# A gated retention and sparse-attention block on one core: another order for the first stage

## The chip, the cores and the metric

The kernel runs on one core of a Trainium2 chip. The metric is the device time of one execution in microseconds (us); lower is better. The kernel before took 1618.48 us, the median of three runs (1618.11 to 1619.36).

## The reference

One decoder layer on x, 512 tokens of 2048 channels, in fp32. What the change touches is the beginning and the last step:

```python
mod = silu(c) @ w_ada + b_ada                 # one row of 6144 from w_ada, 2048 x 6144
shift, scl, gate = split(mod, 3)
h = rmsnorm(x, g_norm) * (1 + scl) + shift
(..., n_kc, ..., n_ks, ..., n_kw, ...) = split(h @ w_in, ...)
y_ret = retention(rope(r_q), rope(r_k), r_v) * silu(r_g)
y_nsa = nsa_attention(rope(n_q), n_kc, n_vc, rope(n_ks), n_vs, rope(n_kw), n_vw, ...) * silu(n_g)
merged = sigmoid(m_a) * (y_ret @ w_up_ret) + sigmoid(m_b) * (y_nsa @ w_up_nsa)
out = rmsnorm(x + gate * (merged @ w_out), g_final)
```

So nothing can be multiplied by w_in before shift and scl of at least the first channels are known, and these need the whole contraction over c with w_ada.

## The kernel before

The 2048 channels stand on 16 tiles of 128 partitions (kk = 0 to 15), the 512 tokens beside each other. Each factor of a product is split into a high and a low part in fp32r (whi and wlo of the weights, hhi and hlo of h), so that one tile pair takes three matmuls of 128 x 512: hi by hi, hi by lo, lo by hi. Below, such a matmul is called a product.

**Weights.** All weights come over SyncE's queue (SP) in slices of half a megabyte, 128 x 1024, in the order of a list, `plan`; `load` issues what lies up to 12 places ahead (L236), as soon as one of its buffers is free: five `raw` tiles, and two pairs in a pool that is used later for something else. `split` (L251) copies a slice to whi on ScalarE (ACT, L261) and subtracts it to wlo on VectorE (DVE, L262), three of each at a time. Small constants come over GpSimd's queue (POOL) at the start.

**The first stage.** Sixteen squares (DVE, L271) are summed by 16 matmuls against ones (`ssq`, L272); from that comes 1/rms of each token (`rstd_of`, L274, and `rstd_rows`, L289). Beside this, w_ada runs through TensorE (PE) in eight chunks j, each of 512 columns: shift and scl of the two tiles kk = 2j and 2j + 1. A chunk has eight half-megabyte items, two to a batch: `ada_batch` (L316) makes four matmuls of 128 x 512 in fp32 into `pa` (L324). At a chunk's end `xn` (L856) multiplies two tiles of x by 1/rms, `ada_rows` copies `pa` out (ACT), `ada_cols` (L331) turns the row into columns by four matmuls (`misc`, L311; "the column sums" below), adds the constants (`sh`, L337 to L339), makes h (L344), casts it to hhi (ACT, L345) and subtracts to hlo (DVE, L346).

**What fills the gaps.** Two groups of w_in are multiplied meanwhile: group 0 (the keys and values to be compressed) in four PSUM banks, by `Group.steps` (L394, products at L414), 24 products to an item; and group 1 (four key columns of 128, "keys"), item by item into a free bank and added to an fp32 tile `kacc` (`k_step`, L870: products L879, add L885; at the last item the add is L889 and the rope of the column follows it, L486 to L494). The keys come in half-width items of their own array (`w_half`): an item serves two columns over four kk, 12 products to a step. `queue_item` puts steps into a queue `todo` with the batch from which they may run (4j + 2 for chunk j), and `pop` takes steps worth 12 products after each batch: one chunk's products run during the next chunk's sums. `early_splits` splits the next items, up to three ahead, when they are loaded; after the last chunk it runs before every step and takes the first item of the next group (group 2, the values, "v"; its products stand at L414 too, with the weights as the moving side named first, g<-whi,hhi). After the fourth step of that rest `make_gates` (L352) follows: 16 matmuls (`pbg`, L357), and after the eighth 4 more (`pgt`, L364) and the step `gate` on DVE (L368).

**The end.** `out_evac` (L1050) takes the last product's blocks from PSUM, adds the residual, sums the squares (ACT, L1056), and after the fourth block of a row makes its 1/rms by a chain of small steps and writes the row.

Of the kernel before, what the change touches and what calls it, by code (L numbers as in the profile page):

```python
# [85 lines left out]
def block_kernel(ctx: ExitStack, tc: tile.TileContext, t_in, out):  # L86
# [34 lines left out]

    def load_const(name, shape, dt=F32, q=None):
        t = cst.tile(shape, dt, name=f"c_{name}")
        (q or nc.gpsimd).dma_start(t, t_in[name])
        return t
# [6 lines left out]
    gn = load_const("gn", [P, NK])  # L132
    bsh = load_const("bsh", [P, NK])
    bsc = load_const("bsc", [P, NK])
    rtmp = bigt("rtmp")
    bgw = rtmp[:, 7, :].rearrange("p (k c) -> p k c", k=NK)
    nc.gpsimd.dma_start(bgw, t_in["bgw"])
    invc = load_const("invc", [P, 2])
    posb = wk.tile([P, S], I32, tag="pT", bufs=3, name="posb")
    nc.gpsimd.dma_start(posb, bcast(t_in["pos"], S))  # L140
# [29 lines left out]
    def startup_items(j):  # L170

        its = [("w", "in", 0, j)]
        if j % 2:
            its += [("h", 0, j // 2), ("h", 1, j // 2)]
        return its
# [22 lines left out]
    SRC = {"a": "w_ada", "h": "w_half", "in": "w_in", "c": "w_c1", "g": "w_gate", "up_r": "w_ur", "up_n": "w_un", "out": "w_o"}  # L198
    raws, splits = {}, {}
    loaded = [0]  # L200
    w_idx = [i for i, it in enumerate(plan) if it[0] in "wh"]
# [13 lines left out]
    free = {"raw": RAWB, "kv": 2}  # L215
    pair_left = {}

    def load(idx):

        while loaded[0] < min(idx + 12, len(plan)):  # L220
            i = loaded[0]
            it = plan[i]
            if it[0] == "a" and it[2] % 4 >= 2:
                if it[2] % 2 == 0:
                    if not free["kv"]:
                        break
                    free["kv"] -= 1
                    t = kvp.tile([P, 2, 1024], F32, tag="kv", name=f"raw{i}")
                    nc.sync.dma_start(t, t_in["w_ada"][it[1], it[2]:it[2] + 2].rearrange("s p f -> p s f"))
                    raws[i], raws[i + 1] = t[:, 0, :], t[:, 1, :]  # L230
            else:
                if not free["raw"]:
                    break
                free["raw"] -= 1
                r = wp.tile([P, 1024], F32, tag="raw", bufs=RAWB, name=f"raw{i}")
                nc.sync.dma_start(r, raw_src(it))  # L236
                raws[i] = r
            loaded[0] += 1

    def take(i):  # L240

        if i not in raws:
            load(i)
        it = plan[i]
        if it[0] == "a" and it[2] % 4 >= 2:
            free["kv"] += it[2] % 2
        else:
            free["raw"] += 1
        return raws.pop(i)

    def split(upto):  # L251

        while split_ptr[0] < min(upto + 1, len(w_idx)):
# [8 lines left out]
            nc.vector.tensor_tensor(lo, r, hi.bitcast(F32), op=OP.subtract)  # L262
# [5 lines left out]
    for kk in range(NK):  # L268
        sq = wk.tile([P, 512], F32, tag="ev", bufs=4, name=f"sq{kk}")
        xk = xT[kk // 8][:, kk % 8, :]  # L270
        nc.vector.tensor_tensor(sq, xk, xk, op=OP.mult)  # L271
        nc.tensor.matmul(ssq, ones, sq, start=kk == 0, stop=kk == NK - 1)  # L272
# [15 lines left out]

    def rstd_rows():  # L289

        for t in range(NT):
            nc.vector.scalar_tensor_tensor(rtmp[:, 1, :P], ssq[:, t * P:(t + 1) * P], 1.0, ident, op0=OP.mult,
                                           op1=OP.mult, accum_out=st4[:, t:t + 1])
        rstd_of(st4, st4, 1.0 / D, "rr", [P, NT])
        prs = sbank("prs")
        for t in range(NT):
            c = slice(t * P, (t + 1) * P)
            nc.vector.tensor_scalar(rtmp[:, 2, c], ident, st4[:, t:t + 1], None, op0=OP.mult)
# [4 lines left out]
    h_hi = [bigt(f"hhi{a}", F32R) for a in range(2)]  # L303
    h_lo = [bigt(f"hlo{a}", F32R) for a in range(2)]
# [11 lines left out]
    def ada_batch(idx, j, b):  # L316


        load(idx + 1)
        rs = [take(idx + n).rearrange("p (a b) -> p a b", a=2) for n in range(2)]  # L320
        if b == 0:
            pa[j] = tbank(f"pa{j}")
        for u in range(4):
            nc.tensor.matmul(pa[j][32 * u:32 * u + 32, :], sc32[:, 4 * b + u, :], rs[u // 2][:, u % 2, :],  # L324
                             start=b == 0, stop=b == 3)

    def ada_rows(j):
        rows = wk.tile([P, 512], F32, tag="p", bufs=3, name=f"rows{j}")
        nc.scalar.copy(rows, pa.pop(j))
        return rows  # L330

    def ada_cols(j, rows):

        for q in range(4):
            misc_mm(pcol[:, j, q:q + 1], rows[:, q * P:(q + 1) * P], ones[:, 0:1])
        sh = wk.tile([P, 4], F32, tag="sh", bufs=2, name=f"sh{j}")
        nc.vector.tensor_tensor(sh[:, 0:2], pcol[:, j, 0:2], bsh[:, 2 * j:2 * j + 2], op=OP.add)  # L337
        nc.vector.tensor_tensor(sh[:, 2:4], pcol[:, j, 2:4], bsc[:, 2 * j:2 * j + 2], op=OP.add)
        nc.vector.scalar_tensor_tensor(sh[:, 2:4], sh[:, 2:4], 1.0, gn[:, 2 * j:2 * j + 2], op0=OP.add, op1=OP.mult)  # L339
        for u in range(2):  # L340
            kk = 2 * j + u
            a, k8 = divmod(kk, 8)
            h = xT[a][:, k8, :]
# [43 lines left out]
    class Group:  # L387
# [6 lines left out]
        def steps(self, items):  # L394
# [4 lines left out]
            ks = [(self.kk + n * per + u, i, u) for n, i in enumerate(items) for u in range(per)]  # L399
            self.kk += per * len(items)  # L400
            last = self.kk == self.nk

            def step(t):
# [12 lines left out]
                if t == nt - 1:  # L416
# [14 lines left out]
    def run_group(grp, idx, n, between=None, tail=2):  # L431
# [3 lines left out]
        while done < n:  # L435
            if plan[idx][0] not in "wh":
# [9 lines left out]
        while idx < len(plan) and plan[idx][0] not in "wh":  # L446
# [409 lines left out]
    xn_next = [0]  # L856

    def xn(n):

        for _ in range(n):  # L860
            kk = xn_next[0]
            if kk < NK:
                h = xT[kk // 8][:, kk % 8, :]
                nc.vector.tensor_tensor(h, h, rstd, op=OP.mult)
                xn_next[0] += 1

# [4 lines left out]
    def k_step(i, n, t):  # L871
# [3 lines left out]
        for u in range(4):  # L875
            kk = 4 * n + u
            f = slice(u * 256 + (t % 2) * P, u * 256 + (t % 2) * P + P)
            for m, (l, r) in enumerate(((whi[:, f], hhi(kk)), (whi[:, f], hlo(kk)), (wlo[:, f], hhi(kk)))):
                nc.tensor.matmul(b, l, r, start=u == 0 and m == 0, stop=u == 3 and m == 2)  # L879
        if t % 2:  # L880
            splits.pop(i)
        if n == 0:
            nc.scalar.copy(kacc[t], b)
        elif n < 3:
# [11 lines left out]
    def early_splits(idx):  # L896
        while len(splits) < 3 and split_ptr[0] < len(w_idx) and w_idx[split_ptr[0]] <= idx and w_idx[split_ptr[0]] < loaded[0]:
            split(split_ptr[0])

    def queue_item(i, ready):  # L900

        it = plan[i]
        if it[0] == "w":
            todo.extend((ready, 6, f) for f in g0.steps([i]))
        else:
            todo.extend((ready, 12, lambda t=t: k_step(i, it[2], t)) for t in (2 * it[1], 2 * it[1] + 1))
# [263 lines left out]
```

## Time and profile before

| | |
|---|---|
| median of three runs | 1618.48 us |
| the profiled execution, its own time | 1619.62 us |
| its span in the profile | 1617.9 us |
| PE busy | 1588.0 us (98%) |
| DVE, ACT, POOL busy | 712.6 (44%), 489.2 (30%), 33.9 us |
| DMA | 252.54 MB, 156 GB/s over the span |
| granted clock, mean | 0.996 |

The profiled execution is 1.14 us above the median, and 1.72 us of its time lie outside the span. PE is busy nearly throughout; its idle time adds up to 30 us, and the slices of the page show it in the first slice (0 to 40 us) and the last.

### The profile page before, as it was taken

The numbers are of one execution on the slowest core, as the hardware profiler recorded it, in microseconds if no ns is written. First come the engines' busy times: TensorE is split into PE (matmuls) and PEld (weight loads), VectorE is DVE, ScalarE is ACT, GpSimd is POOL, SyncE is SP. The second block draws the span as 40 slices with busy tenths as digits, with TensorE's granted clock in tenths as the row PEclk, the third lists the DMA queues.
The fourth block names the chain that finished last, engine by engine and source line by source line (L and its number), as shares of the span: only waits on it lengthen the run. The fifth ranks groups of instructions, "written<-read, shape, count | busy, mean of one in ns | idle before, by whom it ended". The sixth has DMA issues, their size and how long they took to land.

```text
span 1617.9 us, 18828 instructions
## 1 busy us (share of the span) xinstructions
PE 1588.0 (98%) x7502; PEld 1266.3 (78%) x7502; DVE 712.6 (44%) x1238; ACT 489.2 (30%) x719; POOL 33.9 (2%) x68
## 2 busy tenths in 40 slices
PE   7999999999999999999999999999999999999997
PEld 2566777888888888778888888888888888778886
DVE  5454533345534344542245343332221566654444
ACT  1223313234433534432333333332222222222223
POOL 2000000000000000000001000000001000010000
PEclk9999999999999999999999999999999999999999
DMA  9886354323323313213544554333335777884322
GB/s 373 325 312 222 112 172 152 105 91 106 103 72 98 105 59 98 92 59 111 172 143 134 178 179 147 122 124 124 112 112 167 271 230 236 260 297 182 104 79 105
DMA packets 88217, 252.54 MB, mean 156 GB/s; under 512 B 9248, under 2 KB 18528, under 8 KB 86976
## 3 DMA queue, kind: packets, MB, share of 16 engines
q1 hardware_dynamic: 80048, 235.71, 42.5%
q0 software_dynamic: 7504, 13.53, 2.7%
q10 hardware_dynamic: 576, 2.10, 0.3%
q8 instruction: 59, 0.97, 0.2%
q14 instruction: 30, 0.25, 0.0%
HBM read 224.03 MB, written 27.26 MB: 155 GB/s over the span
## 4 chain that ended last, share of the span: by engine, by line
PE 90%; DVE 4%; DMA 3%; ACT 2%; issue 1%; SPq 0%; ACTq 0%; DVEq 0%
PE g L414 58%; PE o L414 11%; PE u L414 6%; PE g L879 2%; PE o L719 2%; PE sc L682 2%; PE pa L324 2%; PE tp L705 1%; PE ssq L272 1%; PE phid L603 1%; DMA raw<-in_w_ada 1%; DVE wlo L262 1%; DMA raw<-in_w_un 1%; DMA raw<-in_w_ur 1%; PE o L716 1%
## 5 line engine op out<-in xcount | busy, mean ns | idle before, releaser
L262 DVE TENSOR_TENSOR wlo<-raw,whi 128x1024 fp32r<-128x1024 f32 x246 | 297.9, 1223 | 487.0 <-ACT whi L261 486.9
L414 PE MATMUL g<-hhi,whi 128*128 128x512 f32 x1088 | 438.2, 403 | 0.0
L414 PE MATMUL g<-hhi,wlo 128*128 128x512 f32 x1088 | 424.8, 390 | 1.6 <-DVE wlo L262 1.6
L414 PE MATMUL g<-hlo,whi 128*128 128x512 f32 x1088 | 424.1, 390 | 0.0
L261 ACT CAST whi<-raw 128x1024 fp32r<-128x1024 f32 x246 | 255.0, 1048 | 499.8 <-PE g L414 229.0
L414 PEld LDWEIGHTS g<-hhi,whi 128*128 128x128 f32 x1088 | 204.7, 188 | 56.2 <-issue 11.6
L414 PEld LDWEIGHTS g<-hhi,wlo 128*128 128x128 f32 x1088 | 204.5, 188 | 46.4 <-DVE wlo L262 2.5
L414 PEld LDWEIGHTS g<-hlo,whi 128*128 128x128 f32 x1088 | 204.8, 188 | 42.9 <-issue 1.4
L414 PE MATMUL g<-whi,hhi 128*128 128x512 f32 x320 | 133.8, 418 | 0.0
L414 PE MATMUL g<-wlo,hhi 128*128 128x512 f32 x320 | 124.9, 390 | 1.2 <-DVE wlo L262 1.2
L414 PE MATMUL g<-whi,hlo 128*128 128x512 f32 x320 | 125.0, 391 | 0.0
L414 PE MATMUL o<-whi,mhi 128*128 128x512 f32 x240 | 95.0, 396 | 0.0
L414 PE MATMUL o<-wlo,mhi 128*128 128x512 f32 x240 | 93.5, 390 | 0.0
L414 PE MATMUL o<-whi,mlo 128*128 128x512 f32 x240 | 93.4, 389 | 0.0
L414 PEld LDWEIGHTS g<-wlo,hhi 128*128 128x128 f32 x320 | 60.2, 188 | 16.7 <-issue 2.4
L414 PEld LDWEIGHTS g<-whi,hhi 128*128 128x128 f32 x320 | 60.1, 188 | 15.8 <-issue 3.2
L414 PEld LDWEIGHTS g<-whi,hlo 128*128 128x128 f32 x320 | 60.0, 188 | 13.0
L685 DVE CUSTOM_DVE_ANT_0 p<-sc,c_mask 128x128 f32<-128x128 f32 (+3 forms) x64 | 31.2, 488 | 85.3 <-PE sc L682 85.2
L706 ACT COPY pT<-tp 128x128 f32<-128x128 f32 (+3 forms) x64 | 27.3, 426 | 114.6 <-PE tp L705 114.4
L687 ACT ACTIVATE p<-p,sm 128x128 f32<-128x128 f32 (+3 forms) x64 | 36.1, 563 | 75.6 <-DVE sm L685 75.5
L414 PEld LDWEIGHTS o<-wlo,mhi 128*128 128x128 f32 x240 | 45.0, 188 | 10.6 <-issue 1.0
L719 PEld LDWEIGHTS o<-pT,vt 128*128 128x128 f32 x320 | 44.8, 190 | 10.9 <-issue 5.3
(238 smaller groups left out, 1699.8 us busy)
## 6 DMA issues: line engine op xcount, KB each, us to landing
raw<-in_w_in SPq DMA_DIRECT2D x176, 512.0 KB, 3.7
raw<-in_w_ada SPq DMA_DIRECT2D x32, 512.0 KB, 7.7
raw<-in_w_ada SPq DMA_DIRECT2D x16, 1024.0 KB, 8.1
raw<-in_w_gate SPq DMA_DIRECT2D x32, 512.0 KB, 4.7
raw<-in_w_o SPq DMA_DIRECT2D x32, 512.0 KB, 4.4
raw<-in_w_c SPq DMA_DIRECT2D x16, 512.0 KB, 4.1
raw<-in_w_un SPq DMA_DIRECT2D x16, 512.0 KB, 5.1
sg<-ma_d SPq DMA_DIRECT2D x32, 256.0 KB, 3.5
```

What stands on the lines that cost most here:

```text
L261: nc.scalar.copy(hi, r)
L262: nc.vector.tensor_tensor(lo, r, hi.bitcast(F32), op=OP.subtract)
L272: nc.tensor.matmul(ssq, ones, sq, start=kk == 0, stop=kk == NK - 1)
L324: nc.tensor.matmul(pa[j][32 * u:32 * u + 32, :], sc32[:, 4 * b + u, :], rs[u // 2][:, u % 2, :], start=b == 0, stop=b == 3)
L414: nc.tensor.matmul(self.banks[t], l, r, start=kk == 0 and n == 0, stop=kk == self.nk - 1 and n == 2)
L603: nc.tensor.matmul(hid[64 * v:64 * v + 64, :], wins[v, s][:, i, :], craw[v][:, i, :], start=s == 0 and i == 0, stop=s == 7 and i == 3)
L682: nc.tensor.matmul(b[:, :n], qT[:, h, t], res["kT"][:, 2 * br + g, :n], start=True, stop=True)
L685: nc.vector.tensor_tensor_reduce(p[:, :n], b[:, :n], mask[:, 512 - n:], -SCALE, 3.0e38, OP.add, OP.min, sm[:, 0:1])
L687: nc.scalar.activation(p[:, :n], p[:, :n], AF.Exp, bias=sm[:, 0:1], scale=-1.0, accum_out=sm[:, 1:2])
L706: nc.scalar.copy(pT[:, :n], b[:, :n])
L719: nc.tensor.matmul(o[:, r * P:(r + 1) * P], res["v"][:, m, 256 * br + P * g:256 * br + P * g + P], pT[:, m * P:(m + 1) * P], start=k == fi ...
L879: nc.tensor.matmul(b, l, r, start=u == 0 and m == 0, stop=u == 3 and m == 2)
```

## The change

The first stage is written anew.

- **Buffers.** 17 slots of half a megabyte: the five `raw` tiles, four from the two pairs, and eight halves of two large tiles (`xw`) which later become the second half of h (hhi1, hlo1); these eight are given up from the first item of chunk 3 on. `load` runs up to 20 items ahead. The constants that are not needed at once come over SP's queue at the start of chunk 2.
- **First chunk.** Chunk 0 is summed in two halves, of one tile kk each, and the first half's h is made before the second half's sums are run. Its eight items come as 16 DMAs of 256 KB whose rows are 4 x 512 bytes.
- **1/rms.** Of four squares three are on ACT; they are added in pairs on DVE, so that 8 matmuls sum them. The chain to 1/rms stands right behind.
- **Batches.** Chunks 0 and 1 in four batches, the others in two of four items (eight matmuls each).
- **Keys.** Full-width items, two kk for four columns: four steps of 6 products to an item. `w_half` is gone; as many bytes come with `w_in`.
- **Order of the queue.** `pop` takes 24 products after the first batch of a chunk, 18 after the second, and 6 ahead of the column sums. `early_splits` splits up to the item `lim`, which after the last chunk is the last item of group 1.
- **The end.** In `out_evac` the sum of three blocks' squares is made at the third block, so that after the fourth two small DVE steps fewer follow.

The core of the diff:

```diff
+    BATCH = [[2, 2, 2, 2]] * 2 + [[4, 4]] * 6
     for j in range(8):
-        for b in range(4):
-            plan += [("a", j, 2 * b), ("a", j, 2 * b + 1)]
-            if j:
-                plan += startup_items(j - 1)[b:b + 1]
-    plan += startup_items(7)
+        for u in range(8):
+            plan.append(("a", j, u))
+            if (j, u) == (0, 3):
+                plan.append(("w", "in", 0, 0))
+        plan += [("w", "in", g, j) for g in range(2) if j or g]
...
-    free = {"raw": RAWB, "kv": 2}
+    xw = [kvp.tile([P, 2, 1024], F32, tag="kv", name=f"xkv{a}") for a in range(2)]
+    xw += [bigt(f"xw{a}").rearrange(...) for a in range(2)]
+    slots = deque([("raw", None)] * RAWB + [("kv", xw[a][:, u, :]) for a in range(2) for u in range(2)]
+                  + [("big", xw[2 + a][:, u, :]) for a in range(2) for u in range(4)])
...
+            if it[0] == "a" and it[1] == 0:
+                hb, n = divmod(it[2], 4)
+                for u in range(2):
+                    nc.sync.dma_start(r[:, 512 * u:512 * u + 512].rearrange("p (k c) -> p k c", k=4),
+                                      t_in["w_ada"][0, 2 * n + u].rearrange("p (k c) -> p k c", k=4)
+                                      [:, :, P * hb:P * hb + P])
...
-        nc.vector.tensor_tensor(sq, xk, xk, op=OP.mult)
-        nc.tensor.matmul(ssq, ones, sq, start=kk == 0, stop=kk == NK - 1)
+        for u in range(3):
+            nc.scalar.activation(sq[u], xk[u], AF.Square)
+        nc.vector.tensor_tensor(sq[3], xk[3], xk[3], op=OP.mult)
+        for u in (0, 2):
+            nc.vector.tensor_tensor(sq[u], sq[u], sq[u + 1], op=OP.add)
+            nc.tensor.matmul(ssq, ones, sq[u], start=a == 0 and u == 0, stop=a == 3 and u == 2)
...
+    def early_splits():
+        while len(splits) < 3 and w_idx[split_ptr[0]] < min(loaded[0], lim[0]):
+            split(split_ptr[0])
...
+            if b == nb - 1:
+                rows = ada_rows(j)
+                lim[0] = idx + 1
+            pop(24 // nb if j == 1 else 48 // nb if b < nb - 1 else 42 // nb - 6)
...
+        pop(6)
+        cols_mm(j, rows, (0, 1))
+        cols_h(j, (0, 1))
+        for i in (idx, idx + 1):
+            queue_item(i)
+        idx += 2
+        lim[0] = idx
     gates_finish = None
-    for i in range(idx, idx + 3):
-        queue_item(i, 0)
-    idx += 3
     i = 0
     while todo:
-        load(idx - 3)
-        early_splits(idx)
-        todo.popleft()[2]()
+        load(idx - 2)
+        early_splits()
+        todo.popleft()[1]()
...
-                sm = wk.tile([P, 1], F32, tag="fsm", bufs=2, name=f"fsm{t}")
-                nc.vector.tensor_reduce(sm, acc[:, t, :], axis=AX.X, op=OP.add)
-                rstd_of(rf[:, t:t + 1], sm, 1.0 / D, "fr", [P, 1])
+            if j == 2:
+                nc.vector.tensor_reduce(v, acc[:, t, 0:3], axis=AX.X, op=OP.add)
+                nc.vector.tensor_scalar(v, v, 1.0 / D, EPS, op0=OP.mult, op1=OP.add)
+            if j == 3:
+                nc.vector.scalar_tensor_tensor(v, acc[:, t, 3:4], 1.0 / D, v, op0=OP.mult, op1=OP.add)
```

`cols_mm` and `cols_h` do what `ada_cols` did, for one tile kk or for two; `cols_h` begins with the two multiplies of `xn`.

How the order moves is read from the programs' instructions, engine by engine. First, TensorE at a chunk's end in the kernel before: the column sums (misc) of a row, the next chunk's first sums (pa), and then a key step (g_0_2).

```order
L311 MATMUL misc<-ones,rows_892 128x1 x4
L324 MATMUL pa_910<-raw_818,rtmp 32x512 x2
L324 MATMUL pa_910<-raw_841,rtmp 32x512 x2
L879 MATMUL g_0_2_919<-hhi_180,whi_824 128x512
L879 MATMUL g_0_2_919<-hlo_182,whi_824 128x512
```

And the same place in the changed program, at the end of chunk 6; g_3_5 is the last step of chunk 5's keys, g_0_196 the first of chunk 6.

```order
L336 MATMUL misc<-ones,rows_950 128x1 x4
L353 MATMUL pa_0_1012<-raw_937,rtmp 32x512 x2
L353 MATMUL pa_0_1012<-raw_939,rtmp 32x512 x2
L353 MATMUL pa_0_1012<-xkv_118,rtmp 32x512 x2
L353 MATMUL pa_0_1012<-xkv_119,rtmp 32x512 x2
L907 MATMUL g_3_5_1025<-hhi_759,whi_902 128x512
...
L907 MATMUL g_3_5_1025<-hhi_759,wlo_903 128x512
L453 MATMUL g_0_196<-hhi_759,whi_952 128x512
```

Before, a whole chunk of older products stood behind the column sums; now eight sums and six products do, and then those products that need the tiles just made.

Second, VectorE where the first stage gives way to group v, in the kernel before; wlo_1112 and wlo_1204 are the low parts of v's first and second item, kacc_193 to kacc_196 the four key columns.

```order
L368 TENSOR_SCALAR gate_185<-gates,c_valid_101 128x8
L262 TENSOR_TENSOR wlo_1112<-raw_975,whi_1111 128x1024
L889 TENSOR_TENSOR kacc_193<-g_0_3_1115,kacc_193 128x512
L492 TENSOR_TENSOR kT<-kacc_193,cosT 128x512
...
L889 TENSOR_TENSOR kacc_196<-g_3_3_1178,kacc_196 128x512
L492 TENSOR_TENSOR kT<-kacc_196,cosT 128x512
L493 TENSOR_TENSOR rotk_1192<-rotk_1192,sinT 128x512
L494 TENSOR_TENSOR kT<-kT,rotk_1192 128x512
L262 TENSOR_TENSOR wlo_1204<-raw_1019,whi_1203 128x1024
```

The same place in the changed program; wlo_1257 is the low part of v's first item.

```order
L917 TENSOR_TENSOR kacc_203<-g_2_7_1216,kacc_203 128x512
L531 TENSOR_TENSOR kT<-kacc_203,cosT 128x512
L532 TENSOR_TENSOR rotk_1224<-rotk_1224,sinT 128x512
L533 TENSOR_TENSOR kT<-kT,rotk_1224 128x512
L405 TENSOR_SCALAR gate_193<-gates,c_valid_96 128x8
L917 TENSOR_TENSOR kacc_204<-g_3_7_1237,kacc_204 128x512
L531 TENSOR_TENSOR kT<-kacc_204,cosT 128x512
L532 TENSOR_TENSOR rotk_1245<-rotk_1245,sinT 128x512
L533 TENSOR_TENSOR kT<-kT,rotk_1245 128x512
L270 TENSOR_TENSOR wlo_1257<-raw_1118,whi_1256 128x1024
L270 TENSOR_TENSOR wlo_1261<-raw_1122,whi_1260 128x1024
```

The low part of v's first item stood ahead of the four ropes and now stands behind them, and so does the step `gate`.

Third, TensorE from the last sum of squares to the first product, in the changed program (pa_0_235 and pa_4_284 are the two halves of chunk 0).

```order
L288 MATMUL ssq<-sq_161,ones 128x512
L353 MATMUL pa_0_235<-raw_205,rtmp 32x256 x4
...
L336 MATMUL misc<-ones,rows_256 128x1 x2
L317 MATMUL prs<-rtmp,ones 128x128 x4
L353 MATMUL pa_4_284<-xkv_118,rtmp 32x256 x8
L453 MATMUL g_0_196<-hhi_189,whi_258 128x512
```

Before, the sums of two whole chunks but for one batch stood ahead of the first product; now there are those of chunk 0 less two of its items.

## Rows read from the trace of the kernel before

**Rows 1.** The page: busy us of the engines, share of the span, instructions.

```profile
PE 1588.0 (98%) x7502; PEld 1266.3 (78%) x7502; DVE 712.6 (44%) x1238; ACT 489.2 (30%) x719; POOL 33.9 (2%) x68
```

**Rows 2.** PE timeline, 20 to 64 us: start, length, line, operation, count.

```profile
22.81 1.92 PE L324 MATMUL pa<-raw,rtmp 128*32 128x512 f32 x16
39.15 0.80 PE L414 MATMUL g<-hhi,whi 128*128 128x512 f32 x1
61.85 1.06 PE L324 MATMUL pa<-raw,rtmp 128*32 128x512 f32 x8
```

**Rows 3.** Groups by line, PE, 7 to 61.85 us: count | busy us, mean ns.

```profile
L414 PE MATMUL g<-hhi,whi 128*128 128x512 f32 x16 | 7.2, 453 | 0.0
```

**Rows 4.** Windows: start:end, length, PE, PEld, DVE, ACT, POOL busy, granted clock, DMA share, GB/s.

```profile
32.00:34.00 2.00, 0.14 (x4) 0.14 (x8) 1.15 (x2) 0.78 (x2) 0.00 (x0) 1.00 1.04 422
36.00:38.00 2.00, 1.93 (x6) 0.38 (x8) 1.93 (x5) 0.00 (x0) 0.00 (x0) 0.50 1.02 420
40.00:42.00 2.00, 2.00 (x7) 1.54 (x7) 0.00 (x0) 0.00 (x0) 0.00 (x0) 0.64 1.03 420
871.00:872.00 1.00, 1.00 (x6) 0.83 (x5) 0.19 (x1) 0.98 (x2) 0.00 (x0) 1.00 1.01 353
872.00:873.00 1.00, 1.00 (x6) 0.84 (x5) 1.00 (x1) 1.00 (x1) 0.00 (x0) 1.00 0.84 242
```

**Rows 5.** Chain that ended last, 160 to 187 us: start, length, what.

```profile
164.74 0.70 DVE kacc L889
...
178.26 1.23 DVE wlo L262
...
179.53 5.51 PE g L414 x23
```

**Rows 6.** DVE timeline, 0 to 40 us; in brackets idle time before, and its releaser.

```profile
6.37 2.50 DVE L271 TENSOR_TENSOR sq<-xT 128x512 f32<-128x512 f32 x4 [3.54 <-DMA xT<-in_xT]
17.43 1.89 DVE L271 TENSOR_TENSOR sq<-xT 128x512 f32<-128x512 f32 x3 [0.69 <-DMA xT<-in_xT]
23.00 0.29 DVE L292 SCALAR_TENSOR_TENSOR rtmp<-ssq,ident 128x128 f32<-128x128 f32 x1 [2.82 <-PE ssq L272]
28.04 1.29 DVE L864 TENSOR_TENSOR xT<-xT,rtmp 128x512 f32<-128x512 f32 x2
```

**Rows 7.** PE timeline, 60 to 205 us.

```profile
78.86 1.05 PE L311 MATMUL misc<-ones,rows 128*128 128x1 f32 x8 [1.16 <-ACT rows L329]
112.11 0.95 PE L311 MATMUL misc<-ones,rows 128*128 128x1 f32 x8
151.73 3.64 PE L357 MATMUL pbg<-xT,rtmp 128*32 128x512 f32 x32
161.69 0.47 PE L879 MATMUL g<-hhi,whi 128*128 128x512 f32 x1
172.47 0.39 PE L879 MATMUL g<-hhi,wlo 128*128 128x512 f32 x1
```

**Rows 8.** DVE and ACT timeline, 110 to 120 us, around the column sums of 112.11.

```profile
113.52 1.28 DVE L864 TENSOR_TENSOR xT<-xT,rtmp 128x512 f32<-128x512 f32 x2
114.72 0.15 DVE L337 TENSOR_TENSOR sh<-misc,c_bsh 128x2 f32<-128x2 f32 x1
115.75 0.62 ACT L345 CAST hhi<-xT 128x512 fp32r<-128x512 f32 x1 [5.78 <-DVE xT L344]
118.24 0.69 DVE L346 TENSOR_TENSOR hlo<-xT,hhi 128x512 fp32r<-128x512 f32 x1 [0.68 <-ACT hhi L345]
```

**Rows 9.** DMA queues, 0 to 60 us: packets, MB, share of 16 engines.

```profile
q0 software_dynamic: 592, 0.94, 5.6%
```

**Rows 10.** ACT and DVE timeline, 1564 to 1618 us.

```profile
1567.77 2.36 DVE L262 TENSOR_TENSOR wlo<-raw,whi 128x1024 fp32r<-128x1024 f32 x2 [0.25 <-ACT whi L261]
1609.32 0.63 ACT L1056 ACTIVATE oe<-xr 128x512 f32<-128x512 f32 x1 [1.35 <-DVE xr L1055]
1611.49 0.16 DVE L281 TENSOR_TENSOR frv<-frv,fry 128x1 f32<-128x1 f32 x1
```

More of the change, by code (lines that the diff above doesn't have):

```diff
@@ L243, in take, with split @@
             load(i)
[L244 to L248, printed above, removed]
+        slots.append(held.pop(i))
         return raws.pop(i)
-    def split(upto):
+    def split(upto, part=None):
         while split_ptr[0] < min(upto + 1, len(w_idx)):
@@ L328, in ada_rows, with cols_mm @@
+    def ada_rows(j, w=512):
         rows = wk.tile([P, 512], F32, tag="p", bufs=3, name=f"rows{j}")
-        nc.scalar.copy(rows, pa.pop(j))
+        nc.scalar.copy(rows[:, :w], pa.pop(j)[:, :w])
         return rows
[L332 to L341, printed above, removed]
+    def cols_mm(j, rows, us):
+        for n, q in enumerate([u + 2 * v for v in range(2) for u in us]):
+            misc_mm(pcol[:, j, q:q + 1], rows[:, n * P:(n + 1) * P], ones[:, 0:1])
@@ new lines, in cols_h @@
+    def cols_h(j, us, between=None):
+        xn(j, us)
+        u0, n = us[0], len(us)
+        sh = wk.tile([P, 4], F32, tag="sh", bufs=2, name=f"sh{j}{u0}")
+        k0 = 2 * j + u0
+        nc.vector.tensor_tensor(sh[:, 0:n], pcol[:, j, u0:u0 + n], bsh[:, k0:k0 + n], op=OP.add)
+        nc.vector.tensor_tensor(sh[:, 2:2 + n], pcol[:, j, 2 + u0:2 + u0 + n], bsc[:, k0:k0 + n], op=OP.add)
+        nc.vector.scalar_tensor_tensor(sh[:, 2:2 + n], sh[:, 2:2 + n], 1.0, gn[:, k0:k0 + n], op0=OP.add, op1=OP.mult)
+        for u in range(n):
+            kk = k0 + u
@@ L392, in __init__, with steps @@
             self.kk, self.k0 = 0, k0
-        def steps(self, items):
+        def steps(self, items, us=None):
             nt = len(self.banks)
@@ L445, in run_group @@
                 items = []
-        while idx < len(plan) and plan[idx][0] not in "wh":
+        while idx < len(plan) and plan[idx][0] != "w":
             between(idx, plan[idx])
@@ L908, in pop @@
-    def pop(batch, room):
-        while todo and room > 0 and todo[0][0] <= batch:
-            _, n, f = todo.popleft()
+        if it[2] == 0:
+            todo.extend((6 if us is None else 3, f) for f in g0.steps([i], us))
+        else:
+            todo.extend((6, lambda t=t: k_step(i, it[3], t)) for t in range(4))
+    def pop(room):
+        while todo and room > 0:
+            early_splits()
+            n, f = todo.popleft()
             f()
             room -= n
-        return room
@@ L916, in block_kernel @@
[L916 to L934 removed]
+    i_w0 = plan.index(("w", "in", 0, 0))
@@ new lines, in block_kernel @@
+    load(0)
+    for b in range(2):
+        ada_batch(2 * b, 0, 2 * b, 2)
+    rows = ada_rows(0, 256)
+    part = []
+    split(0, part)
+    cols_mm(0, rows, (0,))
+    rstd_rows()
+    cols_h(0, (0,))
+    part[0]()
+    queue_item(i_w0, (0,))
+    ada_batch(5, 0, 4, 2)
+    pop(6)
+    ada_batch(7, 0, 6, 2)
+    rows = ada_rows(0, 256)
+    pop(6)
+    cols_mm(0, rows, (1,))
+    cols_h(0, (1,))
+    queue_item(i_w0, (1,))
+    queue_item(9)
+    idx = lim[0] = 10
+    for j in range(1, 8):
+        if j == 2:
+            for dst, src in late:
+                nc.sync.dma_start(dst, src)
+        s0 = 0
+        nb = len(BATCH[j])
+        for b, n in enumerate(BATCH[j]):
+            load(idx)
+            ada_batch(idx, j, s0, n)
+            idx += n
+            s0 += n
+            if b == nb - 1:
+                rows = ada_rows(j)
+                lim[0] = idx + 1
+            pop(24 // nb if j == 1 else 48 // nb if b < nb - 1 else 42 // nb - 6)
+            for _ in range(2):
+                if j > 2 and tables:
+                    tables.popleft()()
+        pop(6)
+        cols_mm(j, rows, (0, 1))
[4 more added lines that the diff above has]
+        lim[0] = idx
```

190 lines of the change are left out of this document (94 added, 96 removed).

## The prediction

> **What bounds the kernel now.** I read the page first: TensorE is busy 1588.0 of 1617.9 us [rows 1], so a change gains only where PE waits, some 30 us in all, or loses by making it wait anew. The PE timeline says where: the first product starts at 39.15, and at 61.85, when chunk 3's sums begin, 48 products are done (16 of each of three kinds) [rows 2, 3]. The windows tell why: between 32 and 34 us PE works 0.14 of 2 us while the DMA runs at its full 422 GB/s [rows 4]. From 61.85 on PE runs almost without a gap (the column sums at 78.86 wait 1.16 us [rows 7]) until the chain of waits shows the change of group: v's second product waits for the low part of its second item, behind four ropes on VectorE, until 179.53 [rows 5].
>
> The sum is made as a timetable of the changed stage, as far as the instant that answers to that 179.53, the second product of v's second item. Behind it both programs do the same until the end.
>
> **Start.** The first quarter of x is there at 6.37, the last at 17.43 [rows 6]. The 0.94 MB of constants [rows 9] no longer mix with it: three quarters, 3.15 MB, at 420 GB/s [rows 4] take 7.5 us, so 13.9. From there three squares on ACT, priced as the same operation at the end, 0.63 each [rows 10], a last square and add on DVE and two passes of PE give 17.4 for the end of ssq, 5.5 earlier than the 23.00 of before [rows 6]. The chain to 1/rms takes 28.04 - 23.00 = 5.0 us as now [rows 6]: 22.5. Then one tile's multiply (half of 1.29, 0.65), the three steps at sh (0.45 from start to start) and the scaling (0.55), and the cast, 0.62 [rows 6, 8]: first product at 24.8, 14.3 earlier.
>
> **To chunk 3's sums, by PE.** From the order, 90 products are done by then instead of 48. A product costs 0.228 us: from 161.69 to 172.47 lie 47 [rows 7], 10.78 / 47 = 0.229, pauses included. 90 make 20.5. A batch of four matmuls into pa takes 1.06 [rows 2] and 0.14 of changing over; what is left of chunk 0 and the 32 of chunks 1 and 2 make 10.4. Three lots of column sums at 0.5, 0.95 and 0.95 [rows 7]: 2.3. That is 24.8 + 33.2 = 58.0. To it come waits, 1.05 at each of three boundaries (below), 3.15, and the clock. PE will have idled for most of the time from 17.4 to 24.8. Before, after the idle stretch at 32 to 36 us, the granted clock was 0.50 from 36 to 38 and 0.64 on the mean from 40 to 42, so half (1.2 GHz) up to about 41.4 [rows 4]: 5.4 busy us at half rate, a loss of 2.7. The price here lies between 0 and 2.7; PE has somewhat more to do in its idle stretch than it had then, so I take 2.3. Chunk 3's sums begin at 63.4.
>
> **The same, by DMA.** x (4.2 MB), the constants and 34 half-megabyte items make 22.95 MB. Of these 4.2 MB come in rows of 512 bytes; the nearest rows, loads of such rows late in the kernel, moved 353 GB/s in a full window [rows 4]: 11.9 us. The other 18.75 MB at 420: 44.7. Started at about 3.9 (6.37 less one quarter's 2.5) they are in at 60.5. PE is the later of the two. So the change stands 42 products ahead and 1.5 us behind: 8.0 us ahead at this point. `w_half` becoming `w_in` moves no byte and costs nothing.
>
> **Chunks 3 to 7.** Each has 48 products (10.94), two batches of eight sums (2 x 2.07) and column sums (0.88, the row's 0.95 less what overlaps): 15.96. Now the boundary. Counted from the start of the column sums at 112.11, sh starts 2.6 us later (114.72), for an add and the multiplies of xn (1.28) stand ahead of it on DVE; the first hhi is cast at 115.75 (done at +4.3), the second hlo is done at +6.8 [rows 7, 8]. Before, a chunk of older products hid all that. In the new order only eight sums (2.07) and six products (1.37) follow the 0.88 of the column sums, so the first product that needs the new tiles comes at +4.3, that which needs the second tile's at +5.0. With the steps closed up, as no other work is mixed in, I put the second hhi at +5.45 and the second hlo at +6.2: two waits of about 0.5, 1.05 us a boundary. By the row as it stands it is 1.7, and 0 if sh starts a microsecond earlier. 5 x 17.01 = 85.05: the last column sums are through at 148.45.
>
> **The rest of the queue.** 54 products: 6; then a wait without the sums as cover, 1.05 + 2.07 = 3.1; 24 of group 0; `pbg`, 3.64 [rows 7]; and 6 of the first key column. 148.45 + 1.37 + 3.1 + 5.47 + 3.64 + 1.37 + 0.2 until DVE has the bank = 163.6. Before, the first rope's add started at 164.74 [rows 5]. Of the 8.0 us 6.9 are given back by here.
>
> **Into group v.** Before, v's first item was split ahead of the ropes, and its 24 products covered the last of them. Now its low part stands behind the fourth rope. From the first add to the product behind such a subtraction it took 179.53 - 164.74 = 14.79 [rows 5]; `gate`, a small step like the 0.16 of [rows 10], adds 0.25 with its gaps. So v's **first** item gets its second product at 163.6 + 15.05 = 178.6, and the second item's follows 24 products (5.47) later, at 184.1: 4.6 behind the 179.53 of before. PE has 18 key products, `pgt` and one of v in these 15 us, some 5.3, and idles the other 9.7. What is late next is nothing: DVE subtracts v's second and third item while PE multiplies the first.
>
> **Clock.** Such idling brought half rate once [rows 4]; its price is again 0 to 2.7, and I take 2.0. The Trainium skill, "TensorE: Matmul & The Clock Gate", section "HAM oscillation — how this bites in real kernels", says that waits between bursts of matmuls put TensorE back to half rate; the one stretch in these rows agrees, and by it the price would be the whole 2.7, the sum 1625.7.
>
> **End.** Two DVE steps of 0.16 (0.2 with their gaps) go from the last chain [rows 10]: -0.4. Two such steps are put ahead of the low parts at 1567.77 for each of four rows of blocks, 1.5 us on DVE; whether PE then waits no row shows: 0 to +1.5, nearer 0, for those parts are made several items ahead. I take +0.3, together -0.1.
>
> **Sum.** +4.6 + 2.0 - 0.1 = +6.5, against the profiled execution's 1619.62, which is 1.14 above the median of 1618.48: **1625.0**. What a measurement of this kernel can tell from no change is about 0.2%, 3.2 us; so 1615.2 to 1621.7 is the same.
>
> **Rivals.**
> - *h is ready in time* (faster, or the same). If sh starts within 1.6 us of the column sums, the waits at the boundaries vanish: 2.9 up to chunk 3, where the DMA's 60.5 then bounds, 5.25 in chunks 3 to 7, 1.05 behind them, together 9.2. That gives 1615.8, and 1613.8 if the clock keeps its full rate in the tail. For it: in the row the add and xn stand ahead of sh, and a scheduler's order could let them run before the sums end. Against it: the keys' adds double in number (each item now has four columns for every chunk), and the row shows sh 1.7 us behind the end of the column sums. Faster decides from a gain of 9.8: 0.18, and 0.12 for the case with half rate, no change.
> - *The clock keeps its rate* in both stretches, waits as forecast: 1625.0 - 4.3 = 1620.7, the same. For it: 18 products lie spread over the tail's first 8 us. Against it: [rows 4]. 0.16.
> - *The quarter-megabyte halves are slow* (slower still). A neighbouring window with those short rows moved 242 GB/s [rows 4]: 17.3 instead of 11.9 us, the DMA is done at 65.9, 2.5 behind PE: 1627.5. It decides from 300 GB/s down. Against it: in that window the DMA share is 0.84, not full. 0.10. The Trainium skill, "DMA: Bandwidth & Descriptors", section "Rules for kernel authors", wants 1 MiB or more in a DMA for the most bandwidth, which speaks against this part of the change; the half-megabyte loads of before, eight in flight, ran at 420 GB/s all the same [rows 4].
> - *The ropes don't gate v*, because a low part of v stands ahead of them: then the keys' products end at about 168.7, v follows at once, 4.6 becomes -5, the time 1615. DVE's order, with that part behind the last rope, excludes it.
>
> **How the numbers follow.** The forecast with its own spread (1622.7 without the early half rate, 1628.2 with boundaries as the row stands, 0.65 more at five of them) has 0.44, the slow loads 0.10: slower 0.54. Same 0.28, faster 0.18. The range goes from 1615.0 to 1629.0: it takes in the first rival's half-rate case, the slow loads and the full 2.7, and leaves out some 0.12 below and 0.06 above.
>
> **What would show it.** Right: the first product near 25 us; chunks 17.0 apart, with waits of PE for hhi and hlo behind each column sum; v's first low part ending near 178, PE idle for 10 us before it, and half clock behind it. Wrong: column sums 16 us apart with no waits, v's products before 173, or DMA windows under 300 GB/s before 30 us.

## The result, and the profile after

The changed kernel takes 1633.74 us (median of six runs, 1632.80 to 1637.63), the kernel before 1618.45 beside it: a ratio of 1.0099, 95% interval 1.0084 to 1.0113. That is 15.3 us slower between the medians, where 6.5 were forecast (1625.0, at most 1629.0). The profiled execution took 1637.63 us, 18.0 more than the profiled one of before and 3.9 above its own median. So the profile tells a little more than the typical loss. Where the surplus lies shows in two runs below that have the same program up to the rest of the queue and were profiled near their medians (v's items ahead of the ropes, and the gates' bank alone): there it is 1.4 to 1.5 us less from the last column sums to `pbg`.

The page of the changed kernel, busy time: PE has 3.5 us more to do and 14.4 more to wait than in [rows 1].

```profile
span 1635.8 us, 18919 instructions
...
PE 1591.5 (97%) x7518; PEld 1268.9 (78%) x7518; DVE 720.1 (44%) x1253; ACT 496.1 (30%) x732; POOL 28.1 (2%) x57
```

PE timeline, 0 to 70 us (columns as in [rows 2]; in brackets idle time before, and its releaser):

```profile
8.77 3.78 PE L288 MATMUL ssq<-sq,ones 128*128 128x512 f32 x4 [8.77 <-DVE sq L287]
13.93 3.37 PE L288 MATMUL ssq<-sq,ones 128*128 128x512 f32 x4 [1.39 <-DVE sq L287]
18.68 1.98 PE L288 MATMUL ssq<-sq,ones 128*128 128x512 f32 x4 [1.39 <-DVE sq L287]
22.05 1.98 PE L288 MATMUL ssq<-sq,ones 128*128 128x512 f32 x4 [1.39 <-DVE sq L287]
...
31.51 0.50 PE L453 MATMUL g<-hhi,whi 128*128 128x512 f32 x1 [2.07 <-ACT hhi L382]
...
69.11 1.92 PE L353 MATMUL pa<-raw,rtmp 128*32 128x512 f32 x16
```

The four quarters of x are squared and summed strictly one after the other: matmuls, then 1.39 us of squares and adds in which PE waits, then matmuls. The matmuls of the first two quarters also take 3.78 and 3.37 us where those of the last two take 1.98; the granted clock of the windows there is 1.00 (the first of the windows below), so what slows them is not shown. The end of ssq is at 24.0, not at 17.4, and later than the 23.0 of before [rows 6]. The first product comes at 31.5, 7.6 earlier than before, where 14.3 were forecast, and chunk 3's sums begin at 69.1 instead of 61.85 [rows 2], with 42 products more done.

PE timeline at the end of chunk 4 in the changed kernel (102.57 are its column sums):

```profile
102.57 0.95 PE L336 MATMUL misc<-ones,rows 128*128 128x1 f32 x8
...
108.15 0.50 PE L453 MATMUL g<-hhi,whi 128*128 128x512 f32 x1 [0.38 <-ACT hhi L382]
108.88 0.50 PE L453 MATMUL g<-hlo,whi 128*128 128x512 f32 x1 [0.23 <-DVE hlo L383]
```

These are the boundary waits of the forecast: the second hhi and the second hlo come late. From 69.11 to the end of the last column sums at 155.8 (they begin at 154.90, see the next timeline) the five chunks take 86.7 us, 17.3 each (17.0 forecast).

The chain of waits of the changed kernel at the change of group (columns as in [rows 5]):

```profile
173.88 0.70 DVE kacc L917
...
187.74 1.23 DVE wlo L270
...
189.02 11.14 PE g L453 x37
```

And its PE timeline from the last column sums on; `phid` is the first matmul behind v's second item.

```profile
154.90 0.95 PE L336 MATMUL misc<-ones,rows 128*128 128x1 f32 x8
...
158.61 0.51 PE L453 MATMUL g<-hhi,whi 128*128 128x512 f32 x1 [1.27 <-ACT hhi L382]
...
167.25 3.64 PE L394 MATMUL pbg<-xT,rtmp 128*32 128x512 f32 x32
...
178.05 1.05 PE L401 MATMUL pgt<-c_pick,bgrows 128*128 128x32 f32 x8 [1.49 <-DVE kacc L917]
181.34 0.79 PE L907 MATMUL g<-hhi,whi 128*128 128x512 f32 x1 [2.25 <-DVE kacc L917]
...
187.50 0.80 PE L453 MATMUL g<-whi,hhi 128*128 128x512 f32 x1 [3.23 <-ACT whi L269]
...
197.05 0.39 PE L453 MATMUL g<-wlo,hhi 128*128 128x512 f32 x1
...
202.36 1.95 PE L642 MATMUL phid<-raw,kcT 128*64 128x256 f32 x16
```

v's low part does stand behind the fourth rope: from the first rope's add to v's second product it is 15.14 us (15.05 forecast). At the instant with which the sum ends, the second product of v's second item, the changed kernel is at 197.05 and the one before at 179.53 [rows 5]: 17.5 of the profile's 18.0 us lie ahead of it. Below, the start of the first `phid` stands for this place; in the kernel before, the 23 products of [rows 5] end at 185.0.

Windows of the changed kernel (columns as in [rows 4]):

```profile
10.00:12.00 2.00, 2.00 (x3) 0.45 (x2) 0.00 (x0) 1.37 (x3) 0.00 (x0) 1.00 1.00 418
16.00:18.00 2.00, 1.30 (x3) 0.14 (x1) 0.66 (x2) 0.63 (x1) 0.00 (x0) 1.00 1.17 290
34.00:36.00 2.00, 2.00 (x15) 0.85 (x17) 0.00 (x0) 0.00 (x0) 0.00 (x0) 0.50 1.03 410
158.00:160.00 2.00, 1.16 (x3) 0.48 (x3) 1.15 (x2) 0.78 (x2) 0.00 (x0) 1.00 0.00 0
160.00:162.00 2.00, 1.62 (x4) 1.01 (x4) 1.32 (x2) 1.34 (x2) 0.00 (x0) 0.53 0.00 0
184.00:186.00 2.00, 0.27 (x1) 0.00 (x0) 1.58 (x4) 1.04 (x3) 0.00 (x0) 0.50 0.00 0
192.00:194.00 2.00, 2.00 (x6) 1.52 (x6) 1.93 (x7) 0.00 (x0) 0.00 (x0) 0.50 0.90 303
```

The 512-byte rows move 290 GB/s at a DMA share of 1.17, so the engines are full; I had put 353. And the clock falls to half (1.2 GHz) three times: around 34 us, behind the last column sums (not foreseen), and from 181 to 194 us.

### The profile page after: what moved, and what is told of

It reads as the page before. It is cut to its first block, busy times and chain, and to the rows that moved or that the text cites. A ratio compares the mean times of both kernels' runs of the same rounds, so it can differ in the third digit from the quotient of the medians.

```text
span 1635.8 us, 18919 instructions
## 1 busy us (share of the span) xinstructions
PE 1591.5 (97%) x7518; PEld 1268.9 (78%) x7518; DVE 720.1 (44%) x1253; ACT 496.1 (30%) x732; POOL 28.1 (2%) x57
## 4 chain that ended last, share of the span: by engine, by line
PE 85%; DVE 7%; ACT 3%; DMA 3%; issue 2%; SPq 0%; ACTq 0%; DVEq 0%
PE g L453 57%; PE o L453 10%; PE u L453 5%; PE o L758 2%; PE sc L721 2%; PE g L907 1%; DVE wlo L270 1%; PE tp L744 1%; DMA raw<-in_w_ur 1%; PE pa L353 1%; PE phid L642 1%; PE ssq L288 1%; DMA raw<-in_w_un 1%; DVE hlo L383 1%; ACT hhi L382 1%
## 5 line engine op out<-in xcount | busy, mean ns | idle before, releaser
L270 DVE TENSOR_TENSOR wlo<-raw,whi 128x1024 fp32r<-128x1024 f32 x240 | 290.7, 1223 | 510.1 <-ACT whi L269 506.5
L269 ACT CAST whi<-raw 128x1024 fp32r<-128x1024 f32 x240 | 249.0, 1048 | 499.7 <-PE g L453 244.3
L453 PEld LDWEIGHTS g<-hhi,whi 128*128 128x128 f32 x1088 | 205.1, 189 | 63.4 <-ACT hhi L382 11.1
L453 PEld LDWEIGHTS o<-wlo,mhi 128*128 128x128 f32 x240 | 45.0, 188 | 10.9 <-issue 1.0
L758 PEld LDWEIGHTS o<-pT,vt 128*128 128x128 f32 x320 | 44.8, 190 | 10.9 <-issue 5.3
```

What stands on the lines that cost most here:

```text
L269: nc.scalar.copy(hi, r)
L270: low = lambda hi=hi, lo=lo, r=r: nc.vector.tensor_tensor(lo, r, hi.bitcast(F32), op=OP.subtract)
L453: nc.tensor.matmul(self.banks[t], l, r, start=kk == 0 and n == 0, stop=kk == self.nk - 1 and n == 2)
L758: nc.tensor.matmul(o[:, r * P:(r + 1) * P], res["v"][:, m, 256 * br + P * g:256 * br + P * g + P], pT[:, m * P:(m + 1) * P], start=k == fi ...
```

## The experiments

Ratios are to the kernel before, measured beside each run; 0.1% is 1.6 us. The changed kernel stands at 1.0099.

**Eight buffers for the squares.**

```diff
-        sq = [wk.tile([P, 512], F32, tag="ev", bufs=4, name=f"sq{a}{u}") for u in range(4)]
+        sq = [rtmp[:, 2 + u, :] if a % 2 else wk.tile([P, 512], F32, tag="ev", bufs=4, name=f"sq{a}{u}")
+              for u in range(4)]
```

> The squares of every second quarter of x go to four free rows of rtmp, so that squares, adds and matmuls of two quarters can overlap. Theory (the four square buffers chain ACT, DVE and PE, and that chain, not the loads of x, sets the end of ssq at 24.0 us in the changed kernel): ssq ends between 18 and 20 us, the first product comes at 26 to 28 instead of 31.5, and the time falls by 3 to 6 us to about 1629. Rival (the loads with 512-byte rows, which ran at 290 GB/s, bound the start): the first product moves, but chunk 3's sums start at 68 to 69 us as in the changed kernel, and the time falls by less than 1.5 us.

Measured: 1631.44 us, ratio 1.0081 (1.0067 to 1.0095): 2.3 us less by the medians, 2.9 by the ratios, whose intervals overlap. PE timeline, and the window 18 to 20 us:

```profile
8.23 3.78 PE L289 MATMUL ssq<-sq,ones 128*128 128x512 f32 x4 [8.23 <-DVE sq L288]
...
20.39 0.62 PE L354 MATMUL pa<-raw,rtmp 128*32 128x256 f32 x4 [0.28 <-DMA raw<-in_w_ada]
...
27.00 0.50 PE L454 MATMUL g<-hhi,whi 128*128 128x512 f32 x1 [0.20 <-ACT hhi L383]
...
65.04 2.18 PE L354 MATMUL pa<-raw,rtmp 128*32 128x512 f32 x12
67.53 1.05 PE L354 MATMUL pa<-raw,rtmp 128*32 128x512 f32 x4 [0.32 <-DMA raw<-in_w_ada]
```

```profile
18.00:20.00 2.00, 1.93 (x24) 0.72 (x24) 1.48 (x10) 0.21 (x1) 0.00 (x0) 1.00 1.17 290
```

ssq is through at 18.0 and the first product is at 27.0, as the theory of the buffers says: the four buffers did chain the start. The first matmuls are as slow as before (3.78 us), but now run while the next quarter is squared. Chunk 3's sums begin at 65.04 instead of 69.11, so the rival's 68 to 69 is not seen. But PE now waits for loads, which it did not in the changed kernel up to here: 2.7 us in all from 17 to 84 us, the last time among chunk 3's own sums, at 67.53. Of the 4.5 us at the first product the time keeps 2 to 3, a little less than the theory's 3 to 6.

**v's items ahead of the ropes.**

```diff
     i = 0
+    lim[0] = len(plan)
     while todo:
```

> After the last chunk the limit of the early splits is lifted, so that the first two items of group v are split ahead of the ropes; nothing else changes. Theory (v waits for its low part behind the ropes): v's products start right behind the last key step, at 184 us, instead of 187.5 and 189.0, and PE has 48 products to run until the last rope is through; the time falls by 4.7 us if v's first products still run at half rate, by 7.3 if the clock recovers: 1626 to 1629. Rival (PE idles there because of the key steps' PSUM banks and the half clock, the low part is late beside them): the time falls by less than 2 us.

Measured: 1630.08 us, ratio 1.0069 (1.0056 to 1.0081), 3.7 us less by the medians and 4.9 by the ratios, between the two. PE timeline:

```profile
180.51 0.79 PE L907 MATMUL g<-hhi,whi 128*128 128x512 f32 x1 [1.68 <-DVE kacc L917]
...
194.76 1.95 PE L642 MATMUL phid<-raw,kcT 128*64 128x256 f32 x16
```

v follows the last key step at once, without a wait, and `phid` comes at 194.8 instead of 202.4. But that step itself starts at 180.5 only: `pgt` holds one of the two banks of the keys, so the step waits for the third rope's add. The rival's banks are the next thing that is late.

**18 products behind the column sums.**

```diff
-            pop(24 // nb if j == 1 else 48 // nb if b < nb - 1 else 42 // nb - 6)
+            pop(24 // nb if j == 1 else 48 // nb if b < nb - 1 else 3 if j == 2 else 42 // nb - 6)
```

> In chunk 2 twelve products fewer are taken, so that from there on 18 instead of 6 products of older tiles stand behind the column sums; nothing else changes. Theory (the short queue of older products uncovers the chain from the column sums to h at every boundary, 1.2 us a chunk, and 3 us with half rate behind the last one): chunks 3 to 7 are 16.0 to 16.4 us apart instead of 17.3, no wait for hhi or hlo is left, and the time falls by 5 to 9 us to about 1627. Rival (the chunks are long because the second batch's row copy or the weights' splits are late, not the queue): the waits move, the pitch stays above 17, and the time falls by less than 2 us.

Measured: 1649.51 us, ratio 1.0194 (1.0180 to 1.0208): 15.8 us slower than the changed kernel. Both expectations missed. PE timeline:

```profile
83.85 0.95 PE L336 MATMUL misc<-ones,rows 128*128 128x1 f32 x8
...
92.20 0.80 PE L907 MATMUL g<-hhi,whi 128*128 128x512 f32 x1 [2.61 <-DVE kacc L913]
...
103.93 0.95 PE L336 MATMUL misc<-ones,rows 128*128 128x1 f32 x8
```

No hhi or hlo is late any more. But 18 products are three key steps, and the keys have two banks: the third step waits for the first one's add, which the program puts on DVE behind the whole chain to h. Behind that wait the clock is also at half for some 3 us (granted clock 0.50 in the window 92 to 94 us). Chunks are now 20.1 us apart.

**All of it together, and the gates' bank.** The three edits, and

```diff
-            b2 = sbank("pgt")
+            b2 = tbank("pgt")
```

> The edits of the three other runs together, and the eight small matmuls of the block gates go to the bank that pbg left, so that the last key step does not wait behind them for a key's bank. Theory (the three causes add up, less what the loads take back at the start; the bank gives another 3 to 5 us since v follows the keys at 3 us less): v's first product before 165 us and a time of 1609 to 1616, below the kernel before. Rival (the start is bound by the loads, the tail by the ropes): 1620 to 1625, no better than the kernel before.

Measured: 1637.86 us, ratio 1.0121 (1.0107 to 1.0135). A miss for the same reason: the same wait of 2.61 us stands in each chunk. The three other edits are seen to help only against the run before it (11.7 us less).

**12 products behind the column sums.** Two key steps, as many as there are banks: `9 if j == 2` in the line above, alone.

> The changed kernel with 6 products fewer taken in chunk 2, so that 12 products (two key steps) stand behind the column sums instead of 6 (the run with 18 made the third key step wait 2.6 us for the DVE add that stands behind the chain to h). Theory (the boundary waits come from too few older products, and two key steps are what the two key banks bear): no wait for hhi, hlo or kacc behind the column sums, chunks 3 to 7 at 16.2 to 16.6 us instead of 17.3, the time 3 to 6 us below the changed kernel: 1628 to 1631. Rival (any more products behind the sums make DVE's adds queue behind the chain to h): a wait on kacc appears at each boundary and the time is 1634 or more.

Measured: 1626.60 us, ratio 1.0052 (1.0040 to 1.0065), 7 us less than the changed kernel. Column sums in the PE timeline:

```profile
98.70 0.95 PE L336 MATMUL misc<-ones,rows 128*128 128x1 f32 x8
114.60 0.95 PE L336 MATMUL misc<-ones,rows 128*128 128x1 f32 x8
```

That is 15.9 us for a chunk; over chunks 3 to 7 it is 16.3 on the mean (chunk 3 takes 17.3, its first sums drawn out from 1.9 to 3.3 us), as expected; up to the last column sums no wait for hhi or kacc stands behind these sums, and a single one for hlo (0.17 us). So the theory of the uncovered chain stands. The gain is more than expected, and it may not all be the boundaries: in this profile the clock keeps its full rate in the first 60 us, where the same program fell to half around 34 us in the changed kernel's.

**Chunk 0 in whole rows**, on top of the eight buffers; its first two tiles' shift and scl come from wrong columns.

```diff
-                for u in range(2):
-                    nc.sync.dma_start(r[:, 512 * u:512 * u + 512].rearrange("p (k c) -> p k c", k=4),
...
+                nc.sync.dma_start(r, t_in["w_ada"][0, it[2]])
```

> The kernel with eight square buffers, and chunk 0's eight items loaded as they lie, in rows of 4 KB, where the sums expect the halves: the same bytes and instructions but eight DMAs less, so shift and scl of the first two tiles are taken from wrong columns. Theory (once the squares no longer bound the start, the 290 GB/s of the 512-byte rows do, 4.2 MB at 14.4 instead of 10 us): the DMA waits of PE at 20 to 50 and 67 us go, chunk 3's sums start 3 to 4 us earlier than in the run with eight square buffers, and the time is 2 to 4 us lower than its 1631.4. Rival (the loads have slack by chunk 3): less than 1 us.

Measured: 1628.68 us, ratio 1.0068 (1.0056 to 1.0081), 2.8 below the eight buffers by the medians, 2.1 by the ratios, whose intervals overlap. Windows:

```profile
20.00:24.00 4.00, 3.19 (x36) 1.80 (x28) 2.86 (x12) 1.62 (x3) 0.00 (x0) 1.00 1.03 410
24.00:26.00 2.00, 0.18 (x5) 0.06 (x1) 1.25 (x6) 0.62 (x1) 0.00 (x0) 1.00 1.02 406
...
30.00:32.00 2.00, 2.00 (x17) 0.73 (x12) 0.00 (x0) 0.19 (x1) 0.00 (x0) 0.50 1.05 414
```

No wait of PE for a load is left up to chunk 3, and the loads run at 403 to 418 GB/s from 14 to 26 us, when chunk 0 follows x. But chunk 3's sums and `phid` come only 0.5 us earlier: PE, with its sums done sooner, sits idle until h's first tile is ready, and the clock is at half from about 27 to 33 us. In the run with eight buffers alone, fed in small pieces by the loads, it stayed at full rate there. So the price of the short rows in the time is not settled: the medians say 2.8 us, the place says 0.5, and the noise allows either.

**Start and tail without a longer queue:** eight buffers, v's items ahead of the ropes, the gates' bank.

> Eight square buffers, v's first two items split ahead of the ropes, and the block gates' small matmuls in the bank that pbg left; the queue as in the changed kernel. Theory (start and tail are separate causes, and the last key step waits for a bank that the gates' matmuls hold): the last key step starts at about 172 us and v right behind it without waits, first phid matmul at 184 to 187 (202.4 in the changed kernel's profile); the time 1618 to 1622, level with the kernel before. Rival (the half clock returns whatever waits are left): phid at 190 or later, 1625 or more.

Measured: 1620.31 us (11 runs), ratio 1.0018 (1.0009 to 1.0026). PE timeline:

```profile
172.98 0.50 PE L908 MATMUL g<-hhi,whi 128*128 128x512 f32 x1 [0.86 <-DVE kacc L918]
...
185.45 2.44 PE L643 MATMUL phid<-raw,kcT 128*64 128x256 f32 x16
```

As expected: v follows the keys at 174.5, `phid` is at 185.5, where it was before the change, and the clock is 1.00 throughout that stretch. The two edits of the tail are worth 11.1 us on top of the eight buffers by the medians (1631.44 to 1620.31), 10.2 by the ratios. Part of this is clock, and why is not shown: with eight buffers alone it was at half from about 157 to 160 us, and here, behind the same waits of PE, it is not.

**The same with 12 products behind the column sums.**

> As the run before it, with 12 products behind the column sums. Theory (all three causes add up): first phid matmul at 179 to 182, a time of 1613 to 1617, faster than the kernel before by 0.1 to 0.3%. Rival (with the loads as the bound up to chunk 3, the longer queue brings nothing there, or the ropes hold v's third item): equal to the run without it within 1 us.

Measured: 1614.12 us (11 runs), ratio 0.9982 (0.9973 to 0.9991): faster than the kernel before. PE timeline and the window 150 to 180 us:

```profile
167.11 0.50 PE L908 MATMUL g<-hhi,whi 128*128 128x512 f32 x1 [1.15 <-DVE kacc L918]
...
179.57 2.45 PE L643 MATMUL phid<-raw,kcT 128*64 128x256 f32 x16
```

```profile
150.00:180.00 30.00, 28.02 (x138) 19.55 (x137) 22.87 (x36) 12.65 (x17) 0.00 (x0) 1.00 0.20 60
```

As expected. The queue brings 6.2 us more, and up to 1600 us no stretch is left at half rate.

**The gates' bank alone.**

> The changed kernel with nothing but the block gates' small matmuls moved to the bank that pbg left. Theory (v waits for its low part behind the four ropes, whatever the last key step does): the last key step starts 3 to 4 us earlier, v's second product still comes 15 us after the first rope's add, and the time falls by less than 1.5 us. Rival (the keys' bank alone holds v up): v comes 3 to 4 us earlier and the time falls by 3 us or more.

Measured: 1633.55 us, ratio 1.0106 (1.0092 to 1.0120), no gain. PE timeline:

```profile
176.40 0.50 PE L907 MATMUL g<-hhi,whi 128*128 128x512 f32 x1 [0.58 <-DVE kacc L917]
...
185.94 0.79 PE L453 MATMUL g<-whi,hhi 128*128 128x512 f32 x1 [7.91 <-ACT whi L269]
```

The last key step starts 4.9 us earlier (1.5 of them because the half rate behind the last column sums is shorter in this profile), and PE waits 7.91 us for v instead. From the first rope's add to v's second product it is 15.14 us, as in the changed kernel:

```profile
172.32 0.70 DVE kacc L917
...
187.46 8.71 PE g L453 x30
```

So the bank's wait hides behind v's low part, and with that cured it is the next thing late: v's items alone brought about 4 us, the bank alone nothing, both together 10 to 11 on top of the eight buffers.

**The last step alone, in the kernel before.** The new `out_evac`, all else as before.

> The kernel before with the new last step alone (the sum of three blocks' squares made at the third block). Theory (two small DVE steps less at the very end, four pairs more while the fourth column block's weights are split): the last row's chain is 0.3 to 0.4 us shorter, PE waits nowhere more, the time the same within 0.5 us. Rival (the pairs ahead delay the low parts): PE waits for wlo after 1567 us and the time rises by 1 us or more.

Measured: 1618.18 us against 1616.92, ratio 1.0007 (0.9997 to 1.0016). The time is the same by the interval, though not within the 0.5 us expected; from the last block's first DVE step to its scaling it is 4.07 us instead of 4.39, the 0.3 expected. PE has no wait between 1560 us and its last product in either profile, so the rival's wait is not there.

**The fastest kernel with four square buffers again.**

> The fastest kernel so far (eight square buffers, v split early, the gates' bank, 12 products behind the column sums) with the four square buffers back. Theory (of the 5 us by which the chain of squares is late, the loads take back about half by chunk 3): the time rises by 2 to 3 us to 1616 to 1617. Rival (with the queue longer the start is bound by the loads alone): it rises by less than 0.8 us.

Measured: 1615.03 us (11 runs), ratio 0.9987 (0.9978 to 0.9996); the intervals overlap, `phid` is at 180.6 instead of 179.6. About 1 us, between the two expectations: most of what the squares lose at the start is taken back by the loads. The column sums of chunk 2 come 3.9 us later with four buffers (66.71 instead of 62.80), those of chunk 3 only 1.0 (82.88 instead of 81.85), for with eight PE waits for loads among chunk 3's sums (PE timeline of the fastest kernel):

```profile
67.71 1.05 PE L354 MATMUL pa<-raw,rtmp 128*32 128x512 f32 x4 [0.72 <-DMA raw<-in_w_ada]
```

## Why the prediction was wrong

The sign and the mechanisms were right: h too late behind every column sum, v's low part behind four ropes, the half clock in PE's idle stretches. The size was not: 17.5 us at v's second item against 6.6 forecast (4.6 and 2.0 for the clock). By the steps of the forecast, in the changed kernel's own profile:

- **Start: the step that failed.** "A last square and add on DVE and two passes of PE give 17.4 for the end of ssq" took only the last quarter of x, as if the earlier ones were done when it lands. Four buffers for four squares make each quarter wait for the matmuls of the one before, a wait that the forecast put at nothing; the end came at 24.0, 6.6 later, and the first product at 31.5 instead of 24.8. The run with eight buffers shows it: 18.0 and 27.0. About 3.2 of the 6.6 us are the slow matmuls of the first two quarters, which lengthen the chain and which eight buffers hide. I had read in the diff that the squares use four buffers, and did not ask who frees them.
- **To chunk 3's sums:** 69.1 instead of 63.4, so 5.7 of the 6.7 us were left. With eight buffers the sums begin at 65.0, so 4.1 of these are the squares; for the rest the loads, on which PE waits in that run, are the nearest cause, argued and not shown. By DMA I had 353 GB/s for the short rows and "PE is the later of the two". The window of the 353 was a mixture: 145 of its 283 packets were of 2 KB or more. With 290 GB/s PE waits for loads as soon as it does not wait for the squares. The 420 GB/s was read from a mixture too: 1 MB loads stand among the half-megabyte ones of before; those of the changed kernel alone, from 30 to 56 us, ran at 404 to 412.
- **Chunks 3 to 7:** the waits are those forecast, 17.3 instead of 17.0 each, 1.6 us in five. The rival *h is ready in time* was the right way to price them: 9.2 us there, 7 in the run with 12 products behind the sums.
- **The rest of the queue:** 18.1 us from the last column sums to the first rope's add, where 15.15 were forecast. This is the second step that failed, a term put at nothing. The waits were no longer than I had them. The 3.0 us are the clock, at half from about 160 to 167 us (0.53 in the window from 160); I had priced half rate at the start and behind the ropes, and not here, where PE worked 1.16 of 2 us in the window from 158. In the profile of the run with the gates' bank alone the half rate ends at about 164 us, and it is 1.5.
- **Into group v:** 15.14 us against 15.05, as forecast. The `pgt` wait lies inside it and cost nothing by itself, as the run with its bank alone shows.
- **Clock in the tail:** v's first 24 products took 8.03 us (189.02 to 197.05) instead of 5.47: 2.6 against the 2.0 taken, within the forecast's bounds of 0 to 2.7. The clock was at half behind waits of 1.49 and 2.25 us. The Trainium skill ("TensorE: Matmul & The Clock Gate", section "HAM oscillation — how this bites in real kernels") says that waits between bursts of matmuls put TensorE back to half rate; this trace agrees with it, 0.50 in the window from 184 us. In the run with start and tail mended the waits at 155 to 158 us are the same as here behind the last column sums, and the clock stays at 1.00; when it falls is not settled by these runs.
- **End:** -0.1 forecast; the run with this step alone shows the last chain 0.3 us shorter, and in the time no gain and no certain loss.

5.7 + 1.6 + 3.0 + 0.1 + 0.6 = 11.0, the 10.9 us that were missing at v's second item in a profile that is 3.9 us above its median. The run with the gates' bank alone has nearly the changed kernel's median and the same program but for that bank; in its profile the same places give 5.6 + 1.7 + 1.5 + 0.1 - 0.3 = 8.6 us, and the time missed the forecast by 8.7. So the start is most of the miss, but not all: cured alone it leaves 1631.44 us, still above the range's 1629.0.

## What to carry to other kernels

Where a change gives one stage to several engines, write down for each buffer who frees it: four squares in four buffers are a chain of ACT, DVE and PE, not three engines side by side. A backlog of ready products covers a chain only as long as its own results have somewhere to go; here two banks allow two key steps, and a third one turned 7 us of gain into 16 of loss. And before a wait is costed, ask what is late next: the key's bank hid behind v's low part, its cure brought nothing alone, and with v's items early the two brought 10 to 11 us.

## What the runs showed that I had not expected

Loads of 256 KB in rows of 512 bytes at the start of the kernel ran at 290 GB/s with the DMA engines fully busy (share 1.17), those in 4 KB rows in the same place at 403 to 418. And giving PE its data earlier may cost clock: with whole rows PE was idle until h came and then ran at half rate for some 6 us, in the one profile of that run; with the slower loads, which fed it in small pieces, it kept the full rate in all four profiles with eight buffers. That the idle time alone decides is not shown: with four buffers the same start fell to half rate in five profiles and kept the full rate in a sixth.
